# Raw gate weights of the first set in tiles of their own, asked for a pair ahead, in a hybrid decoder step

## The chip, the cores and the metric

The kernel runs on one core of a Trainium2 chip. The metric is the device time of one execution in microseconds; three executions were timed, and one more was taken with the hardware profiler. Engines are named as the profile does: PE is TensorE's matmul side (PEld its weight loads), DVE VectorE, ACT ScalarE, POOL GpSimd, SP SyncE, which here only issues transfers.

## What is computed

One decoder layer, for a prompt of 2048 tokens and for eight single-token samples that continue from given states. The mixer has two groups of four heads, retention (RET) and HGRN2:

```python
h = rmsnorm(x, norm_g)
p = (h @ w_in).astype(jnp.float32)                 # 1024 x 4096
rq, rk, rv, rg, hq, hf, hi, hgate = jnp.split(p, 8, axis=-1)
rq, rk = rotary(rq, pos), rotary(rk, pos) * RET_DK ** -0.5
o_ret, s_ret_new = chunked_decay_recurrence(rq, rk, rv, log_gamma, s_ret)
o_ret = head_rmsnorm(o_ret, ret_g) * silu(rg)
o_hg, s_hg_new = chunked_decay_recurrence(silu(hq), kin, hi, logf, s_hg)   # kin, logf from hf
o_hg = head_rmsnorm(o_hg, hg_g) * silu(hgate)
y = x + concatenate([o_ret, o_hg]) @ w_out
return rmsnorm(y, final_norm_g), new states
```

## The kernel before

All large products are made in fp32 as three passes over a high and a low part (`three`, L350: high x high, high x low, low x high). The first 570 us make the projections `rv`/`hi` (set 0), `rq`/`rg` (set 1) and `rk`/`hgate` (set 2). Each set goes over the prompt in eight chunks of 256 tokens; the loop counter `i` runs from 0 to 23 over all three sets, and the tiles of chunk i are named after it (`pv4a`, `s40h`). Chunks 0 and 1 are plain products. From chunk 2 on each chunk is a chain of seven products of half size with sums of operands (a Strassen-Winograd scheme): A11, A12, S2, S1, S3, S4, A22 against B11, B21, T2, T1, T3, B22, T4 (`CHAIN`). A product is 12 matmuls of 128x512. `v_pair` writes the chain, and the dictionary `after[n]` holds what is put in behind product n (n from 0 to 6; n - 0.5 is its middle). TensorE's order is exactly the order in which the code is written; the other engines' order is made by a scheduler, except where `behind(f)` ties the instructions of f to come after the last ones already issued on VectorE, ScalarE and SP.

The weights of sets 1 and 2 are used twice. While set 0 runs, the raw weights of set 1 (`w_1`, eight k-tiles `wgr` of 128x1024, in four pairs k and k + 4) are loaded by `wg_load` into buffers of the pool `rawp` (six buffers, tag `raw`, shared with the token tiles `xr` and the operand sums `S`); `wg_decode` multiplies them with the sample tokens (`four`, L590: four matmuls of 8x256 per k-tile into `pgd`); `w_sums` makes the T operands in place, and `wg_spool` stores these into `ws1T`, from where the next set fetches them. Set 1 does the same for set 2. Pair k has its place in chunk k + 2: load behind product 0, decode behind product 4 (5 in chunk 3).

Around these stand: `stats_load`/`stats_sum` (tiles `xn`: squares of the prompt rows on ScalarE for the norms; `stats_end` makes `rs_all` on POOL, `spread` transposes it on TensorE, `prs`, and copies it to `rb`); `tok_load`/`tok_ops` (tokens of the next chunk, scaled by `rb`, their high and low parts `ab_h`, `ab_l` and sums `S`); `decode_values` (the sample values from the raw weights `wvr` of set 0, in the plain chunk 0, behind its second and fourth k-pair); `wv_comb` (T operands of set 0, in place in `wvr`, so behind `decode_values`). In set 2 the retention recurrence runs inside the chain (`r_steps`, L797 on): `r_flip` transposes the keys `rk` (`pkt`), `r_score` and `r_update` follow. Later, in the output projection, `wd_at` places the steps of the decode output: `d_ms`, `d_rs` (VectorE's `do`, L1392), `d_tr` (TensorE's transpose `pdt`). `MOVE` shifts single score groups of the HGRN2 part in TensorE's order. The small matmuls `wu` (L84, L86) run while the first loads are under way. Tiles of the pool `vq` have one buffer per tag: `zh0`, `zl0`, `zh1`, `zl1` hold the A21 operands of chunks 0 and 1, `rk` and `rg` are otherwise used from the decode rotation of chunk 7 on.

Of the kernel before, what the change touches and what calls it, by code (L numbers as in the profile page):

```python
# [10 lines left out]
F32 = mybir.dt.float32  # L11
# [3 lines left out]
ALU = mybir.AluOpType  # L15
# [26 lines left out]
def step_kernel(ctx, tc, a, out):  # L42
# [42 lines left out]
    for n in range(12):  # L85
        pe.matmul(wu[:32, :16], ones[:, :32], ones[:, :16], start=True, stop=True)  # L86
# [415 lines left out]
    def w_sums(r0, r1):  # L502
        dve.tensor_tensor(r0[:, 0], r0[:, 1], r0[:, 0], op=ALU.subtract)
        dve.tensor_tensor(r0[:, 1], r1[:, 1], r0[:, 1], op=ALU.subtract)
        dve.tensor_tensor(r1[:, 1], r1[:, 1], r0[:, 0], op=ALU.subtract)
        dve.tensor_tensor(r1[:, 0], r1[:, 0], r1[:, 1], op=ALU.subtract)
        return ("T2", r1[:, 1]), ("T3", r0[:, 1]), ("T1", r0[:, 0]), ("T4", r1[:, 0])
# [6 lines left out]
    def wg_load(n, k):  # L514
        for kk in (k, k + 4):
            wr[kk] = rawp.tile([P, 2, GW], F32, tag="raw", name=f"wgr{n}{kk}")
            sp.dma_start(wr[kk].rearrange("p g n -> p (g n)"), a[f"w_{n}"][kk])
# [3 lines left out]
    def wg_decode(n, k):  # L521
        if n not in pgd:
            pgd[n] = ps_o.tile([P, 256], F32, tag="o", name=f"pgd{n}")
        for kk in (k, k + 4):
            four(pgd[n], xs[:, kk], wr[kk].rearrange("p a b -> p (a b)"), kk == 0, kk == KT - 1)
# [5 lines left out]
    def wg_decode_out(n):  # L531
        t, u = (vq.tile([NB, GW], F32, tag="vo", name=f"gd{n}{ty}", bufs=3) for ty in range(2))
        for ty, x in enumerate((t, u)):
            for m in range(2):
                j = 2 * ty + m
                act.activation(x[:, m * 256 : m * 256 + 256], pgd[n][32 * j : 32 * j + NB], AF.Copy)
        act.activation(u, u, AF.Silu)
        hd = NH * (n - 1)
        sp.dma_start(dg_dram[hd : hd + NH].rearrange("u b d -> b u d"), u.rearrange("b (u d) -> b u d", d=P))
        r = vq.tile([NB, GW], F32, tag="rv", name=f"gdr{n}")  # L540
        rotd = vq.tile([NB, GW], F32, tag="rk", name=f"rotd{n}")[:, :P]
        sp.dma_start(rotd, a["rotd"])
        turn(r, t, rotd, f"d{n}")
        dec_rot[n] = r
# [42 lines left out]
    def four(ps, x, w, first, last):  # L587

        for j in range(4):
            pe.matmul(ps[32 * j : 32 * j + x.shape[1]], x, w[:, j * 256 : j * 256 + 256], start=first, stop=last)  # L590
# [71 lines left out]
    for kk in range(4):  # L662
        for k in (kk, kk + 4):
            for ty in range(2):
                for c in range(2):
                    plain_k(0, pv0[c, ty], c, ty, k, k == 0, k == KT - 1)
        if kk % 2:
            for k in (kk - 1, kk, kk + 3, kk + 4):
                decode_values(k)
# [125 lines left out]
    def r_steps(p):  # L795
# [22 lines left out]
        if p < N_V:  # L818
            put(3, lambda: r_load(ca, "q"), lambda: r_load(ca, "v"))
            d = 0 if p else 0.5  # L820
            put(3.5 + d, lambda: r_flip(ca))
            put(4 + d if p else 6, lambda: r_load(ca, "g"))
# [85 lines left out]
    for i in range(2, n_tok):  # L908
# [30 lines left out]
        if i + 2 < N_V:  # L939
            after[1 if i == 2 else 2] += [lambda i=i: behind(lambda: stats_sum(i + 2, 0)), lambda i=i: stats_load(i + 2, 1)]  # L940
# [8 lines left out]
        if m < 3:  # L949
            if 2 <= j < 6:  # L950
                after[0] += [lambda m=m, k=j - 2: wg_load(m, k)]
                after[5 if i == 3 else 4] += [lambda m=m, k=j - 2: wg_decode(m, k), lambda m=m, k=j - 2: wg_spool(m, k)]
# [224 lines left out]
    MOVE = {(0, 0, 1): 0.065, (0, 1, 3): 0.065, (0, 2, 1): 0.065, (1, 0, 1): 0.125, (1, 3, 1): 0.11}  # L1177
# [699 lines left out]
    wd_at[2] += [(0, d_ms), (2, d_rs), (4, d_tr)]  # L1877
# [103 lines left out]
```

## Time and profile before

| | us |
|---|---|
| median of three runs | 1028.73 (1026.5 to 1032.09) |
| profiled execution, device time | 1030.97 |
| its span, first to last instruction | 1029.1 |
| PE busy | 1014.0 (99%) |
| DVE busy | 734.2 (71%) |
| ACT busy | 550.3 (53%) |
| POOL busy | 122.8 (12%) |
| data moved | 255.63 MB, mean 248 GB/s |

A busy PE means that matmuls are under way; since they overlap, the starts of two following matmuls tell more than their durations. In the timeline a row gives the start and the duration in us, then engine, line, operation and tiles; what stands in brackets is the idle time ahead of it and who ended it.

### The profile page before, as it was taken

How to read it: one execution, taken by the hardware profiler on the slowest of the kernel's cores; microseconds unless marked ns; L12 is line 12 of the kernel's file. 1: busy time of each engine (PE TensorE's matmuls, PEld its weight loads, DVE VectorE, ACT ScalarE, POOL GpSimd, SP SyncE). 2: the span in 40 equal slices, each digit the busy share in tenths (PEclk: the TensorE clock that was granted, in tenths of full speed). 3: DMA queues.
4: the chain of work that ended last, by engine and by line, in shares of the span. 5: the costliest groups of instructions: out<-in, count | busy, mean ns of one | idle time of the engine just before them, and what ended most of it. 6: DMA issues, size and time to landing. Idle time of an engine off the chain costs nothing.

```text
span 1029.1 us, 21541 instructions
## 1 busy us (share of the span) xinstructions
PE 1014.0 (99%) x8366; PEld 841.7 (82%) x8366; DVE 734.2 (71%) x1353; ACT 550.3 (53%) x1211; POOL 122.8 (12%) x231
## 2 busy tenths in 40 slices
PE   9999999999999999999999999999999999999997
PEld 7767778887778888888888899898888878878775
DVE  7887666888675885576666768768768576667886
ACT  7863435735434765555564665667556476433242
POOL 0200001000000101111111100111022112301122
PEclk9999999999999999999999999999999999999999
DMA  8699998878999965567766697555864496565652
GB/s 290 210 327 330 332 334 275 326 263 313 312 326 304 359 238 184 189 226 247 233 222 205 210 334 268 193 185 200 283 216 133 129 362 227 180 252 204 227 186 103
DMA packets 151271, 255.63 MB, mean 248 GB/s; under 512 B 11424, under 2 KB 79280, under 8 KB 151040
## 3 DMA queue, kind: packets, MB, share of 16 engines
q1 hardware_dynamic: 141408, 225.03, 64.7%
q0 software_dynamic: 7440, 24.76, 6.3%
q10 hardware_dynamic: 2320, 4.46, 1.2%
q8 instruction: 66, 1.08, 0.4%
q14 instruction: 37, 0.30, 0.1%
HBM read 166.51 MB, written 87.69 MB: 247 GB/s over the span
## 4 chain that ended last, share of the span: by engine, by line
PE 82%; DMA 4%; DVE 1%; issue 0%; SPq 0%; POOLq 0%; ACT 0%; POOL 0%; DVEq 0%; ACTq 0%
PE po L350 10%; PE pjqh L1032 9%; PE pjfh L1032 8%; PE py L1659 4%; PE plh L1246 2%; PE pur L741 1%; PE par L734 1%; PE puh L1115 1%; PE por L747 1%; PE por L749 1%; PE poh L1131 1%; DMA oT1h<-t_dramh 1%; PE poh L1133 1%; PE pv20a L350 1%; PE pv21a L350 1%; PE pv22a L350 1%
## 5 line engine op out<-in xcount | busy, mean ns | idle before, releaser
L1032 PE MATMUL pjfh<-xh,w_h 128*128 128x512 f32 (+2 forms) x160 | 59.4, 372 | 0.0
L1032 PE MATMUL pjqh<-xh,w_h 128*128 128x512 f32 (+2 forms) x160 | 58.9, 368 | 0.0
L1226 ACT ACTIVATE kepth<-kh 128x1024 f32<-128x1024 f32 x24 | 25.4, 1060 | 62.0 <-DVE kh L1216 62.0
L1032 PE MATMUL pjqh<-xh,w_l 128*128 128x512 f32 (+2 forms) x160 | 55.7, 348 | 0.0
L1032 PE MATMUL pjfh<-xh,w_l 128*128 128x512 f32 (+2 forms) x160 | 55.7, 348 | 0.0
L1032 PE MATMUL pjfh<-xl,w_h 128*128 128x512 f32 (+2 forms) x160 | 55.6, 348 | 0.0
L1032 PE MATMUL pjqh<-xl,w_h 128*128 128x512 f32 (+2 forms) x160 | 55.6, 347 | 0.0
L1216 DVE TENSOR_TENSOR kh<-kh,fph 128x512 f32<-128x512 f32 x48 | 33.4, 696 | 22.8 <-PE plh L1246 19.8
L118 DVE TENSOR_TENSOR ab_l<-xr,ab_h 128x512 fp32r<-128x512 f32 (+1 forms) x40 | 37.5, 954 | 11.6 <-ACT ab_h L117 11.6
L772 DVE SCALAR_TENSOR_TENSOR obr<-por,omr,rg 128x128 f32<-128x128 f32 x64 | 18.0, 344 | 33.3 <-POOL omr L764 28.2
L762 ACT ACTIVATE obr<-por 128x128 f32<-128x128 f32 x64 | 16.8, 277 | 44.4 <-PE por L749 40.6
L117 ACT ACTIVATE ab_h<-xr 128x512 fp32r<-128x512 f32 (+1 forms) x40 | 32.4, 838 | 11.3 <-DVE xr L302 11.3
L1032 PEld LDWEIGHTS pjqh<-xh,w_h 128*128 128x128 f32 x160 | 30.4, 190 | 4.8 <-issue 1.2
L1032 PEld LDWEIGHTS pjfh<-xh,w_h 128*128 128x128 f32 x160 | 30.2, 189 | 4.1 <-issue 0.4
L1032 PEld LDWEIGHTS pjqh<-xh,w_l 128*128 128x128 f32 x160 | 30.1, 188 | 4.1
L1032 PEld LDWEIGHTS pjfh<-xh,w_l 128*128 128x128 f32 x160 | 30.1, 188 | 4.0
L409 ACT ACTIVATE vo<-vo 128x512 f32<-128x512 f32 x32 | 20.1, 629 | 24.7 <-DVE vo L403 10.8
L1219 DVE TENSOR_TENSOR qqh<-qqh,fph 128x512 f32<-128x512 f32 x48 | 32.8, 683 | 0.0
L1032 PEld LDWEIGHTS pjqh<-xl,w_h 128*128 128x128 f32 x160 | 30.2, 189 | 3.0
L1032 PEld LDWEIGHTS pjfh<-xl,w_h 128*128 128x128 f32 x160 | 30.2, 189 | 2.7
L302 DVE SCALAR_TENSOR_TENSOR xr<-xr,g_in,rb 128x256 f32<-128x256 f32 x64 | 27.1, 480 | 7.3 <-DMA xr<-in_x_t 4.2
L1659 PE MATMUL py<-woh,oc_h 128*128 128x512 f32 x64 | 26.6, 415 | 0.0
(1839 smaller groups left out, 3335.0 us busy)
## 6 DMA issues: line engine op xcount, KB each, us to landing
xr<-a_dram SPq DMA_DIRECT2D x24, 512.0 KB
S<-s_dram SPq DMA_DIRECT2D x24, 512.0 KB
xn<-in_x_prompt SPq DMA_DIRECT2D x32, 256.0 KB
xr<-in_x_t SPq DMA_DIRECT2D x16, 512.0 KB
a_dram<-xr SPq DMA_DIRECT2D x16, 512.0 KB
s_dram<-S SPq DMA_DIRECT2D x16, 512.0 KB
wgr<-in_w SPq DMA_DIRECT2D x16, 512.0 KB
xr<-a_dram SPq DMA_DIRECT2D x32, 256.0 KB
```

The source lines that it names most:

```text
L117: act.activation(h, src, AF.Copy)
L118: dve.tensor_tensor(l, src, h.bitcast(F32), op=ALU.subtract)
L302: dve.scalar_tensor_tensor(r[:, k], r[:, k], g_in[:, kk : kk + 1], spread_to[i], op0=ALU.mult, op1=ALU.mult)
L350: pe.matmul(ps, xx, ww, start=(first and n == 0), stop=(last and n == 2), skip_group_check=more)
L409: act.activation(o, src, AF.Silu)
L772: dve.scalar_tensor_tensor(o[:, cc], po[:, h], ms[:, h : h + 1], rb_of[c, "g"][:, cc], op0=ALU.mult, op1=ALU.mult)
L1032: pe.matmul(ps, ww[:, kk], x[:, k, b0 : b0 + n], start=(k == 0 and i == 0), stop=(k == KT - 1 and i == 2),)
L1216: dve.tensor_tensor(kv[:, :, 0, :], kv[:, :, 0, :], two[:, :, 1:2].to_broadcast([P, nb, b]), op=ALU.mult)
L1219: dve.tensor_tensor(qv[:, :, 1, :], qv[:, :, 1, :], two[:, :, 0:1].to_broadcast([P, nb, b]), op=ALU.mult)
L1226: act.activation(ss[:, 512:], k[:, :HALF], AF.Copy)
L1246: pe.matmul(dst[32 * i : 32 * i + 32, c], kk, qq, start=True, stop=True)
L1659: pe.matmul(ps, o[:, kk], w[:, k % 4, i * 512 : (i + 1) * 512], start=(k == 0 and n == 0), stop=(k == KT - 1 and n == 2),)
```

## The change

The raw weights of set 1 no longer share `rawp` for most of their tiles. Pair 0 and pair 2 keep one `raw` buffer for their first k-tile, and the second goes as two halves into the tiles `rk` and `rg`; pairs 1 and 3 go as four halves into `zh0`, `zl0`, `zh1`, `zl1`. Pair 0 is loaded behind product 1 of chunk 2, each further pair behind product 5 of the chunk before its own, and all are decoded behind product 6. `w_sums`, `wg_decode` and `four` take a list of halves. Beside that: the gate store `dg_dram` of set 1 is issued by ScalarE instead of SP; `decode_values` runs in one block behind chunk 0; `stats_sum` and `stats_load` stand behind product 1 in all chunks; the first `r_flip` of set 2, with the first score and update, stands half a product later; `d_tr` moves from product 4 of output block 2 to product 0 of block 3; one score group of head 3 (`MOVE`) moves forward; three more small warm-up matmuls.

```diff
     def w_sums(r0, r1):
-        dve.tensor_tensor(r0[:, 0], r0[:, 1], r0[:, 0], op=ALU.subtract)
...
+        b11, b12, b21, b22 = (r[:, g] if hasattr(r, "shape") else r[g] for r in (r0, r1) for g in range(2))
+        dve.tensor_tensor(b11, b12, b11, op=ALU.subtract)
+        dve.tensor_tensor(b12, b22, b12, op=ALU.subtract)
+        dve.tensor_tensor(b22, b22, b11, op=ALU.subtract)
+        dve.tensor_tensor(b21, b21, b22, op=ALU.subtract)
+        return ("T2", b22), ("T3", b12), ("T1", b11), ("T4", b21)
...
     def wg_load(n, k):
-        for kk in (k, k + 4):
-            wr[kk] = rawp.tile([P, 2, GW], F32, tag="raw", name=f"wgr{n}{kk}")
-            sp.dma_start(wr[kk].rearrange("p g n -> p (g n)"), a[f"w_{n}"][kk])
+        for j, kk in enumerate((k, k + 4)):
+            if n == 1 and (j or k % 2):
+                tags = (f"zh{j}", f"zl{j}") if k % 2 else ("rk", "rg")
+                wr[kk] = [vq.tile([P, GW], F32, tag=t, name=f"wgr{n}{kk}{t}") for t in tags]
+                for g, r in enumerate(wr[kk]):
+                    sp.dma_start(r, a[f"w_{n}"][kk, :, g * GW : (g + 1) * GW])
+            else:
+                wr[kk] = rawp.tile([P, 2, GW], F32, tag="raw", name=f"wgr{n}{kk}")
+                sp.dma_start(wr[kk].rearrange("p g n -> p (g n)"), a[f"w_{n}"][kk])
...
-        sp.dma_start(dg_dram[hd : hd + NH].rearrange("u b d -> b u d"), u.rearrange("b (u d) -> b u d", d=P))
+        (act if n == 1 else sp).dma_start(dg_dram[hd : hd + NH].rearrange("u b d -> b u d"), u.rearrange("b (u d) -> b u d", d=P))
...
-    for n in range(12):
+    for n in range(15):
         pe.matmul(wu[:32, :16], ones[:, :32], ones[:, :16], start=True, stop=True)
...
-        if kk % 2:
-            for k in (kk - 1, kk, kk + 3, kk + 4):
+        if kk == 3:
+            for k in range(KT):
                 decode_values(k)
...
-            d = 0 if p else 0.5
+            d = 0 if p else 1
             put(3.5 + d, lambda: r_flip(ca))
-            put(4 + d if p else 6, lambda: r_load(ca, "g"))
+            put(4 if p else 6, lambda: r_load(ca, "g"))
...
-            after[1 if i == 2 else 2] += [lambda i=i: behind(lambda: stats_sum(i + 2, 0)), lambda i=i: stats_load(i + 2, 1)]
+            after[1] += [lambda i=i: behind(lambda: stats_sum(i + 2, 0)), lambda i=i: stats_load(i + 2, 1)]
...
-                after[0] += [lambda m=m, k=j - 2: wg_load(m, k)]
-                after[5 if i == 3 else 4] += [lambda m=m, k=j - 2: wg_decode(m, k), lambda m=m, k=j - 2: wg_spool(m, k)]
+                if m == 1:
+                    if j == 2:
+                        after[1] = [lambda m=m: behind(lambda: wg_load(m, 0))] + after[1]
+                    if j < 5:
+                        after[5] += [lambda m=m, k=j - 1: behind(lambda: wg_load(m, k))]
+                else:
+                    after[0] += [lambda m=m, k=j - 2: wg_load(m, k)]
+                after[6 if m == 1 else 4] += [lambda m=m, k=j - 2: wg_decode(m, k), lambda m=m, k=j - 2: wg_spool(m, k)]
...
-    MOVE = {(0, 0, 1): 0.065, (0, 1, 3): 0.065, (0, 2, 1): 0.065, (1, 0, 1): 0.125, (1, 3, 1): 0.11}
+    MOVE = {(0, 0, 1): 0.065, (0, 1, 3): 0.065, (0, 2, 1): 0.065, (1, 0, 1): 0.125, (1, 3, 1): 0.11, (0, 3, 1): -0.06}
...
-    wd_at[2] += [(0, d_ms), (2, d_rs), (4, d_tr)]
+    wd_at[2] += [(0, d_ms), (2, d_rs)]
+    wd_at[3] += [(0, d_tr)]
```

`four` and `wg_decode` index these lists instead of slicing one tile; the products are the same.

TensorE, end of chunk 2: before, the decode block of pair 0 (`pgd`, read from `wgr`) stands behind the fifth product, the second on `pv2a` with T3.

```order
L350 MATMUL pv2a<-T3h,s20l 128x512
L350 MATMUL pv2a<-T3h,s20h 128x512
L350 MATMUL pv2a<-T3l,s20h 128x512
L350 MATMUL pv2a<-T3h,s20l 128x512
L590 MATMUL pgd_922<-wgr_791,pk 8x256 x4
L590 MATMUL pgd_922<-wgr_793,pk 8x256 x4
L350 MATMUL pv2c<-B22h,s21h 128x512
L350 MATMUL pv2c<-B22l,s21h 128x512
```

In the change it stands behind the seventh product (T4), ahead of chunk 3, and reads the second k-tile from `wgr14rk` and `wgr14rg`.

```order
L350 MATMUL pv2a<-T4h,ab_h 128x512
L350 MATMUL pv2a<-T4l,ab_h 128x512
L350 MATMUL pv2a<-T4h,ab_l 128x512
L599 MATMUL pgd_969<-wgr_810,pk 8x256 x4
L599 MATMUL pgd_969<-wgr14rk,pk 8x256 x2
L599 MATMUL pgd_969<-wgr14rg,pk 8x256 x2
L350 MATMUL pv3a<-wv_h,ab_h 128x512
L350 MATMUL pv3a<-wv_l,ab_h 128x512
```

The block has moved two products later, with the same sixteen small matmuls.

SP's queue in the same chunk: before, the two loads of pair 0 stand ahead of the store of the first output (`v_dram`).

```order
L324 DMA s_dram_121<-S_2_708 128x1024
L263 DMA xn_761<-in_x_prompt 128x512
L517 DMA wgr_791<-in_w 128x1024
L517 DMA wgr_793<-in_w 128x1024
L344 DMA v_dram_95<-vo_808 128x512
L263 DMA xn_819<-in_x_prompt 128x512
L263 DMA xn_820<-in_x_prompt 128x512
L312 DMA a_dram_114<-xr_716 128x1024
```

In the change pair 0 has three loads and stands behind that store:

```order
L324 DMA s_dram_121<-S_2_711 128x1024
L263 DMA xn_764<-in_x_prompt 128x512
L344 DMA v_dram_95<-vo_807 128x512
L524 DMA wgr_810<-in_w 128x1024
L521 DMA wgr14rk<-in_w 128x512
L521 DMA wgr14rg<-in_w 128x512
L263 DMA xn_824<-in_x_prompt 128x512
L263 DMA xn_825<-in_x_prompt 128x512
```

Pair 1, which stood in chunk 3 before, follows in the same chunk, in four halves:

```order
L344 DMA v_dram_96<-vo_914 128x512
L263 DMA xn_942<-in_x_prompt 128x512
L263 DMA xn_943<-in_x_prompt 128x512
L344 DMA v_dram_96<-vo_939 128x512
L521 DMA wgr11zh_946<-in_w 128x512
L521 DMA wgr11zl_947<-in_w 128x512
L521 DMA wgr15zh_950<-in_w 128x512
L521 DMA wgr15zl_951<-in_w 128x512
L344 DMA v_dram_95<-vo_966 128x512
```

The first loads moved one store later, the second pair about half a chunk earlier.

VectorE at the start: before, the first in-place sums on the raw weights of set 0 (`wvr`, L503 to L506) stand among the splits of the later raw tiles.

```order
L118 TENSOR_TENSOR B12l_220<-wvr_267,B12h_218 128x512
L503 TENSOR_TENSOR wvr_223<-wvr_223 128x512
L503 TENSOR_TENSOR wvr_245<-wvr_245 128x512
L504 TENSOR_TENSOR wvr_223<-wvr_228,wvr_223 128x512
L118 TENSOR_TENSOR T1l<-wvr_223,T1h 128x512
L118 TENSOR_TENSOR wv_l<-wvr_289,wv_h 128x512
L118 TENSOR_TENSOR B12l_220<-wvr_289,B12h_218 128x512
L118 TENSOR_TENSOR wv_l<-wvr_291,wv_h 128x512
```

In the change they stand behind the splits of the tokens of chunk 1 (`x0r`), since TensorE reads the raw tiles for the decode values in one block:

```order
L481 SCALAR_TENSOR_TENSOR ab_l<-x0r_328,g_in,ab_h 128x128
L481 SCALAR_TENSOR_TENSOR a21l_207<-x0r_328,g_in,a21h_206 128x128
L481 SCALAR_TENSOR_TENSOR ab_l<-x0r_330,g_in,ab_h 128x2x128
L504 TENSOR_TENSOR wvr_226<-wvr_226 128x512
L481 SCALAR_TENSOR_TENSOR ab_l<-x0r_330,g_in,ab_h 128x2x128
L505 TENSOR_TENSOR wvr_226<-wvr_231,wvr_226 128x512
L504 TENSOR_TENSOR wvr_248<-wvr_248 128x512
L506 TENSOR_TENSOR wvr_231<-wvr_231,wvr_226 128x512
L118 TENSOR_TENSOR T1l<-wvr_226,T1h 128x512
```

All 32 operations of that kind now follow one another behind the decode block.

## Rows read from the trace of the kernel before

**Rows 1.** The page, busy time of each engine with its share and instructions.
```profile
PE 1014.0 (99%) x8366; PEld 841.7 (82%) x8366; DVE 734.2 (71%) x1353; ACT 550.3 (53%) x1211; POOL 122.8 (12%) x231
```

**Rows 2.** TensorE's waits: us in total, times, longest.
```profile
PE pgd L590 <- DMA wgr<-in_w: 2.7, 5, 0.7
PE pkt L726 <- DVE rk L375: 1.4, 1, 1.4
PE pdt L1396 <- DVE do L1392: 1.2, 1, 1.2
...
PE prs L288 <- POOL rs_all L114: 0.6, 1, 0.6
PE pv2b L350 <- DVE ab_l L118: 0.4, 1, 0.4
PE pv2a L350 <- ACT s L390: 0.3, 1, 0.3
```

**Rows 3.** The chain that ended last, in chunk 6: start, us, twelve matmuls.
```profile
143.63 2.72 PE pv6a L350 x12
```

**Rows 4.** Timeline of TensorE around the first and the last stalled decode block.
```profile
70.80 0.39 PE L350 MATMUL pv2a<-T3h,s20l 128*128 128x512 f32 x1
...
73.35 0.50 PE L350 MATMUL pv2c<-B22h,s21h 128*128 128x512 f32 x1
...
135.69 0.39 PE L350 MATMUL pv5a<-T3h,s50l 128*128 128x512 f32 x1
...
137.88 0.50 PE L350 MATMUL pv5c<-B22h,s51h 128*128 128x512 f32 x1
```

**Rows 5.** The same around an unstalled decode block of the second set.
```profile
236.80 0.39 PE L350 MATMUL pv10a<-T3h,s100l 128*128 128x512 f32 x1
...
238.09 0.50 PE L350 MATMUL pv10c<-B22h,s101h 128*128 128x512 f32 x1
```

**Rows 6.** Timeline of SP's issues, last pair of the first set.
```profile
128.22 1.32 SPq L517 DMA_DIRECT2D wgr<-in_w  x2
```

**Rows 7.** Timeline of TensorE, transpose of the norms in chunk 4.
```profile
104.67 0.39 PE L350 MATMUL pv4b<-wv_h,ab_l 128*128 128x512 f32 x1
...
105.63 0.43 PE L288 MATMUL prs<-ident,rs_all 128*128 128x128 f32 x2 [0.58 <-POOL rs_all L114]
```

**Rows 8.** Timeline of TensorE and VectorE, first transpose of keys in chunk 16.
```profile
361.85 0.39 PE L350 MATMUL pv16a<-T3h,s150l 128*128 128x512 f32 x1
363.65 0.63 PE L726 MATMUL pkt<-ident,rk 128*128 128x128 f32 x4 [1.41 <-DVE rk L375]
...
362.81 0.69 DVE L375 TENSOR_TENSOR rk<-t,t 128x512 f32<-128x512 f32 x1
```

**Rows 9.** Timeline of TensorE, transpose of the decode output.
```profile
914.50 0.39 PE L350 MATMUL po<-woh,op2S1l 128*128 128x512 f32 x1
916.07 0.24 PE L1396 MATMUL pdt<-ident,do 64*128 64x64 f32 x1 [1.18 <-DVE do L1392]
```

**Rows 10.** Timeline of VectorE and TensorE, first sums and second decode block.
```profile
19.59 1.28 DVE L503 TENSOR_TENSOR wvr<-wvr 128x512 f32<-128x512 f32 x2
20.79 0.68 DVE L504 TENSOR_TENSOR wvr<-wvr,wvr 128x512 f32<-128x512 f32 x1
...
31.49 1.91 PE L590 MATMUL pvd<-wvr,pk 128*8 128x256 f32 x32
```

**Rows 11.** Timeline of VectorE and TensorE, tokens of chunk 2 and its first matmul.
```profile
50.21 0.42 DVE L290 COPY rb<-prs 128x256 f32<-128x256 f32 x1 [1.34 <-PE prs L288]
...
53.86 0.69 DVE L118 TENSOR_TENSOR ab_l<-xr,ab_h 128x512 fp32r<-128x512 f32 x1 [0.72 <-ACT ab_h L117]
...
55.51 0.39 PE L350 MATMUL pv2a<-wv_h,ab_h 128*128 128x512 f32 x1
```

**Rows 12.** DMA from 60 to 140 us; stretch of chunk 6, DMA share second to last.
```profile
DMA packets 10211, 27.08 MB, mean 339 GB/s; under 512 B 1151, under 2 KB 1151, under 8 KB 10205
...
143.20:163.30 20.10, 20.10 (x91) 16.50 (x91) 13.24 (x24) 8.25 (x14) 1.08 (x3) 1.00 0.84 285
```

More of the change, by code (lines that the diff above doesn't have):

```diff
@@ L502, in w_sums @@
     def w_sums(r0, r1):
-        dve.tensor_tensor(r0[:, 0], r0[:, 1], r0[:, 0], op=ALU.subtract)
[L504 to L507, printed above, removed]
+        b11, b12, b21, b22 = (r[:, g] if hasattr(r, "shape") else r[g] for r in (r0, r1) for g in range(2))
[4 more added lines that the diff above has]
+        return ("T2", b22), ("T3", b12), ("T1", b11), ("T4", b21)
     def wv_comb(k):
@@ L524, in wg_decode @@
         for kk in (k, k + 4):
-            four(pgd[n], xs[:, kk], wr[kk].rearrange("p a b -> p (a b)"), kk == 0, kk == KT - 1)
+            halves = wr[kk] if isinstance(wr[kk], list) else [wr[kk][:, g] for g in range(2)]
+            four(pgd[n], xs[:, kk], halves, kk == 0, kk == KT - 1)
     def wg_spool(n, k):
@@ L589, in four @@
         for j in range(4):
-            pe.matmul(ps[32 * j : 32 * j + x.shape[1]], x, w[:, j * 256 : j * 256 + 256], start=first, stop=last)
+            ww = w[j // 2] if isinstance(w, list) else w[:, j // 2 * 512 : j // 2 * 512 + 512]
+            pe.matmul(
+                ps[32 * j : 32 * j + x.shape[1]], x, ww[:, j % 2 * 256 : j % 2 * 256 + 256], start=first, stop=last
+            )
     pvd = []
```

## The prediction

> **What bounds the kernel now.** I read the page's busy table first: TensorE is busy for 1014.0 us, 99% of the span [rows 1]. A change that takes no matmul out can only win from the 15 us in which TensorE stands, so the next view is TensorE's own list of waits [rows 2]. It has few: 2.7 us in five waits for the raw gate weights (`wgr`, read by the small decode products at L590), one wait each for a transpose of `rk` (1.4), a transpose of the decode output (1.2) and a transpose of the norms `rs_all` (0.6), and two at the start of the first chained chunk (0.4 and 0.3). The list shows idle time by modelled ends of matmuls; the price of a wait I take from starts in the timeline instead. Large matmuls follow each other at 2.72/12 = 0.227 us [rows 3]; what a stretch takes beyond that and beyond its normal small work is lost.
>
> **The change, part by part.**
>
> *Raw weights earlier (L514 to L525, L951).* Before, pair k of the first gate set is requested at the head of its chunk and consumed behind the fifth or sixth product of the same chunk. From the last large matmul ahead of a decode block to the first behind it took 2.55 us in the first block and 2.19 in the last stalled one; the stalled one between them took 2.65, by the same two rows of its place [rows 4]. In the second set the same 16 small matmuls cost 238.09 - 236.80 = 1.29 us unstalled [rows 5]. So the three stalls cost 2.55 + 2.65 + 2.19 - 3 x 1.29 = 3.5 us; the fourth block, pair 1's, did not wait. The last pair's requests stand on SP's queue from 128.22 on, and the block that waited for them ended at 137.88, so a transfer takes some 9 us from issue here [rows 4, 6]. After the change pair 0 is asked for some 2 us later on SP (one store now stands ahead of it) but consumed two products later (2 x 2.72 = 5.4 us), which leaves 3 us against waits below 1 us; pairs 1 to 3 are asked for a chunk (about 20 us) ahead. The new tiles (`rk`, `rg`, `zh0` to `zl1`) are free: the early chunks have finished with the `z` tiles when chunk 2 starts at 55.51 [rows 11], and the two sets alternate, so a load waits on SP only for the stores of the sums two pairs back. Such a wait may take a few us; the loads themselves have 20 us, but the `xn` loads stand behind them on SP (rival A). Saving 3.5 us, at least 2.5 (first and last block only), none if the queue is the limit (a rival below). The same 4 MB move either way. SP issues 14 loads instead of 8.
>
> *The statistics one product earlier (L940).* The transpose of `rs_all` that waits stands in chunk 4; the last squares that it needs stand on ScalarE behind the first copy of `pv4a`, which waits for TensorE. The order after puts them ahead of that copy. Loss before: 105.63 - 104.67 - 0.23 = 0.73 us [rows 7]. I take 0.7, bounds 0 and 0.7. It also pulls `xn` squares forward on ScalarE for the later chunks; if an `xn` load is late, the PSUM copies queue behind it.
>
> *The first transpose of keys half a product later (L820, L821).* Before, it stood 363.65 - 361.85 - 0.23 = 1.57 us for VectorE's rotation, which ends at 362.81 + 0.69 = 363.50 [rows 8]. Six large matmuls (1.36 us) now come ahead of it, so TensorE arrives at 363.44 on that clock and waits at most 0.2. The score behind it moves by the same six, so its distance stays. Saving 1.3, bounds 1.0 and 1.57.
>
> *The decode output's transpose two products later (L1877).* Loss before: 916.07 - 914.50 - 0.23 = 1.34 us [rows 9]. It moves by some 36 large matmuls (8 us); VectorE's product for it stays where it is. Saving 1.3; no lower bound below 1.2 that the rows suggest.
>
> *Decode values in one block (L667), three more tiny warm-up matmuls (L85).* The work is the same, one switch fewer: nothing. But the first four raw tiles are now read by TensorE until about 31 us, so VectorE's in-place sums on them cannot begin at 19.59, as they did, but at about 29.9 [rows 10] (the second block of 32 small matmuls began at 31.49; the 64 now begin 1.9 earlier, at 29.6). 32 operations (16 sums, 16 low parts) at 0.60 us each are 19.3 us, so the end is 49.2 if nothing waits. Before, `rb`, which follows them, ran at 50.21 waiting for TensorE, and the first block's low part was done at 54.55 for matmuls that start at 55.51 (the third of these reads it) [rows 11]. If ScalarE makes VectorE wait for about 2 us, the low part is done at 56.5 and TensorE loses about 0.5. On the other side SP now issues more of the statistics loads ahead of the two 512 KB token loads, so ScalarE may wait less, and both waits of this place (0.4 and 0.3 of idle time, [rows 2]) can go; with the restart behind each, which cost the decode blocks up to a third more than the idle time, that is some 1 us. I take a loss of 0.5; bounds: a gain of 1.0 and a loss of 2.0, the whole lateness. The warm-up adds six records of a 32x16 product; the second real matmul waits for its split behind it anyway: nothing.
>
> *Score group of head 3 earlier (`MOVE`), gate store on ScalarE's queue (L539).* No wait of [rows 2] lies at either, so neither gives anything; if the score group came too early, it would cost one wait of the size of [rows 8] at worst. The store leaves SP; what it gives is sequencer time on a queue that nobody waits for there. The Trainium skill ("DMA: Bandwidth & Descriptors", section "Issuing engines are not separate DMA queues") says the same: transfers run on the same 16 engines whoever issues them. By it, too, nothing is to be had.
>
> **Sum.** -3.5 - 0.7 - 1.3 - 1.3 + 0.5 = -6.3 us. The profiled execution took 1030.97 us, 1.87 beyond its span and 2.24 above the median of the three runs; taken off the median, 1028.73 - 6.3 = **1022.4 us**, 0.6% less. Half a per cent (5.1 us) is about what a measurement of this kernel can tell from no change, so the forecast stands just beyond it.
>
> **Rivals.**
>
> *A. The DMA queue is the limit, and the stalls move.* From 60 to 140 us the queue moved 27.08 MB at 339 GB/s; in chunk 6 behind it, at 285 GB/s, the DMA engines' share is 0.84 [rows 12], so 339 is close to all they do with such transfers (285/0.84 = 339). Without the stalls the stretch takes about 4.2 us less (3.5 + 0.7) and wants 27.08/75.8 = 357 GB/s. If it can't have them, token or `xn` loads come late and TensorE or ScalarE waits for these instead, until the slack behind 143 us. For it: the load. Against: pairs 1 to 3 now have 20 us, tokens are used a chunk after they are asked for, and backlog of a few us drains at 0.84. Price: the 4.2 us, leaving -2.1: 1026.6. Chance 0.17.
>
> *B. The start is late.* As bounded above, 2.0 instead of 0.5: -4.8, 1023.9. For it: the sums that began at 19.59 cannot fill VectorE's time there any more. Chance 0.18.
>
> *C, slower. Shorter rows slow the queue itself.* Six of the eight raw loads become pairs of 256 KB with 2 KB rows instead of 4 KB. That is 768 packets more on 10211 [rows 12], 7.5%. If each packet had a fixed price, the rate would fall; the other terms give 2.1 us, so the kernel gains nothing once the stretch takes 82.1 us instead of 80 (330 GB/s), and is slower by 0.5% at 87.2 us (311 GB/s). At 300 GB/s it takes 90.3 us, 8.2 more than it can: 1036.9. Against: the stretch already consists of 256 KB and 512 KB transfers and reaches 339. Chance 0.04. The Trainium skill speaks for C ("DMA: Bandwidth & Descriptors", section "Rules for kernel authors": 1 MiB and more per transfer; "Perfetto Trace Analysis", section "DMA Optimizations": going from 2 KB to 4 KB can improve throughput a lot). The first page's section "Bandwidth" gives 341 GB/s for a single 1 MB transfer; this trace has 339 with transfers of a quarter to a half of that in a full queue. By the rule the time would go towards C's 1036.9, by the row halving costs nothing, and I go by the row.
>
> *D. The change doesn't reach the waits*: the loads land no earlier because `behind` and the scheduler hold them. The order speaks against it (pair 1's loads stand half a chunk earlier): 0.03. Then the 3.5 us stay: 1028.73 - 2.8 = 1025.9.
>
> **Chances.** Forecast 0.58, A 0.17, B 0.18, C 0.04, D 0.03. Three runs before spread from 1026.5 to 1032.1, so a median is good to some 2 us: of the forecast about 0.70 falls beyond 5.1 us, of B 0.45, of A 0.2. That gives faster 0.41 + 0.08 + 0.03 = 0.52, slower 0.04, the same 0.44. Range: best 1028.73 - 6.3 - 1.5 (the start gains 1.0) = 1020.9, less some 2 for the median: 1018.5; top end A plus 1: 1027.6.
>
> **What the profile after would show.** The five waits for `wgr` gone and each decode block near 1.3 us; no wait of `prs` at chunk 4; `pkt` at most 0.2; `pdt` none; TensorE idle down by some 5 us. VectorE's sums starting at about 30 us, `rb` at 50 to 52, and a wait of `pv2a` of 0 to 1 us. A shows as new waits of TensorE for ScalarE or VectorE behind DMA `xr` or `xn` between 80 and 143 us; C as a rate clearly below 339 GB/s in that stretch. The prediction is wrong if TensorE's waits go and the span does not follow, or if waits appear behind 143 us, where I priced nothing.

## The result and the profile after

The changed kernel takes 1031.47 us (median of 22 runs, 1027.37 to 1037.52), the kernel before in the same comparison 1028.35 us (22 runs): 1.0031 times as long, 95% interval 1.0019 to 1.0043. That is some 3 us slower, less than the half per cent that the prediction called telling, but clear by the interval; 1022.4 us was forecast and 1027.6 was the top of the range.

The execution whose trace was read first took 1037.52 us, 6 us above the median. So the changed kernel was profiled once more (1030.74 us; run e12 below), and the kernel before as well (1025.78 us; run e5). TensorE's waits in this second profile of the changed kernel (us in total, times, longest):

```profile
PE pv8a L350 <- ACT s L390: 1.8, 1, 1.8
PE plh L1263 <- issue: 1.2, 1, 1.2
PE wu L84 <- POOL ones L78: 1.1, 1, 1.1
PE pv2c L350 <- ACT p L390: 1.0, 1, 1.0
PE pv2a L350 <- ACT ab_h L117: 0.6, 1, 0.6
PE par L745 <- DMA rq<-qt_dram: 0.4, 1, 0.4
PE pv2a L350 <- ACT s L390: 0.3, 1, 0.3
PE pv2b L350 <- DVE ab_l L118: 0.2, 1, 0.2
```

Against [rows 2] every wait that the change was to remove is gone: none for `wgr`, `prs`, `pkt` or `pdt`. Others stand in their place. Two of the new ones are the largest that both profiles of the changed kernel share: `pv8a` in chunk 8, the first chunk of set 1, and `pv2c` in chunk 2. In the first profile of the changed kernel the place of `pv8a` cost more; TensorE's timeline there:

```profile
185.45 0.49 PE L350 MATMUL pv8b<-wv_h,ab_h 128*128 128x512 f32 x1 [0.72 <-ACT wv_h L117]
...
186.71 0.50 PE L350 MATMUL pv8b<-wv_l,ab_h 128*128 128x512 f32 x1 [0.77 <-DVE wv_l L118]
...
190.21 0.79 PE L350 MATMUL pv8a<-T2h,s70h 128*128 128x512 f32 x1 [2.06 <-ACT s L390]
```

A stretch of the same profile (us; busy times of PE, PEld, DVE, ACT and POOL; granted clock, DMA share, GB/s):

```profile
190.00:195.00 5.00, 4.79 (x15) 3.84 (x16) 5.00 (x5) 4.26 (x6) 0.00 (x0) 0.67 1.04 411
```

There are three waits, 3.55 us together, and from the end of the last of them on TensorE has a piece at the lower clock level (1.2 GHz instead of 2.4; the granted clock is 0.92 on average from 189 to 190 us, 0.50 from 190 to 193 and 0.67 from 190 to 195). It is no single case: the mean granted clock of the whole execution is 0.996 or less in 12 of the 22 executions of the changed kernel and in 1 of the 116 of the kernel before that ran beside the experiments.

Because TensorE runs nearly without a gap, the account is best kept by the time from the first matmul of one chunk to the first of the next. Worked out from TensorE's timelines, in us, where the four profiles differ:

| stretch | before, 1030.97 | before, 1025.78 | changed, 1037.52 | changed, 1030.74 |
|---|---|---|---|---|
| start to chunk 2 | 55.51 | 56.04 | 56.47 | 56.08 |
| chunk 2 | 23.43 | 20.92 | 23.88 | 23.93 |
| chunk 4 | 22.64 | 21.82 | 20.50 | 20.50 |
| chunk 5 | 21.38 | 21.37 | 20.50 | 20.50 |
| chunk 8 | 20.10 | 20.09 | 25.95 | 22.19 |
| chunk 16 | 23.99 | 22.72 | 22.45 | 22.44 |
| chunk 17 to output projection (`py`) | 467.22 | 466.93 | 467.63 | 468.87 |
| output projection on `po`, to its end | 120.97 | 119.77 | 121.47 | 119.84 |

The mean of the two profiles of before against the second of the changed kernel: chunks 4 and 5 gain 1.7 + 0.9, chunk 16 gains 0.9, the output projection 0.5; chunk 2 loses 1.75, chunk 8 2.1 (5.9 in the first profile of the changed kernel), the start 0.3. So the gains are 4.0 us instead of 6.8 (the stalled decode block of chunk 2 is not among them: what it gave back is part of that chunk's net loss), and they are lost again at the start, in chunk 2 and in chunk 8 even in the milder of the two executions. Of the 1.8 between chunk 17 and the output projection 0.4 are for `par` and 1.2 at `plh`; a run without any of the weights' part (e11) has 1.6 at `plh` too, so I count that to the spread of executions, which is not shown further.

The two profiles of before also differ from each other, and in places that the prediction summed. TensorE's waits in the second:

```profile
PE pgd L590 <- DMA wgr<-in_w: 1.0, 2, 0.7
PE prs L288 <- POOL rs_all L114: 0.8, 2, 0.6
```

And its timeline at `pkt` and `pdt`:

```profile
359.47 0.39 PE L350 MATMUL pv16a<-T3h,s150l 128*128 128x512 f32 x1
359.98 0.63 PE L726 MATMUL pkt<-ident,rk 128*128 128x128 f32 x4
...
910.62 0.39 PE L350 MATMUL po<-woh,op2S1l 128*128 128x512 f32 x1
910.94 0.28 PE L1396 MATMUL pdt<-ident,do 64*128 64x64 f32 x1
```

`pkt` stands 0.51 - 0.23 = 0.28 us there instead of the 1.57 of [rows 8], `pdt` 0.1 instead of 1.34 [rows 9], and `wgr` 1.0 instead of 2.7 [rows 2].

### The profile page after: what moved, and what is told of

Same layout as the page of the kernel before. It is cut to its first block, busy times and chain, and to the rows that moved or that the text cites. A ratio compares the mean times of both kernels' runs of the same rounds, so it can differ in the third digit from the quotient of the medians.

```text
span 1035.7 us, 21567 instructions
## 1 busy us (share of the span) xinstructions
PE 1017.9 (98%) x8372; PEld 843.1 (81%) x8372; DVE 734.6 (71%) x1353; ACT 551.2 (53%) x1211; POOL 126.9 (12%) x231
## 5 line engine op out<-in xcount | busy, mean ns | idle before, releaser
L409 ACT ACTIVATE vo<-vo 128x512 f32<-128x512 f32 x32 | 20.1, 628 | 23.7 <-DVE vo L403 10.5
```

The lines of the kernel that those rows point to most:

```text
L409: act.activation(o, src, AF.Silu)
```

## The experiments

Medians are of 11 or 12 runs each (6 for e15; e5 and e12 are one execution each), with those of before taken beside them (1027.96 to 1028.12, 23 to 35 runs); the ratio to before is given with its 95% interval. Edits are shown against the changed kernel unless said otherwise.

**e1: the statistics put back.**
```diff
-            after[1] += [lambda i=i: behind(lambda: stats_sum(i + 2, 0)), ...
+            after[1 if i == 2 else 2] += [lambda i=i: behind(lambda: stats_sum(i + 2, 0)), ...
```


> The changed kernel with one edit undone: the squares for the statistics stand again behind step 2 of a chunk (step 1 in chunk 2). Theory T (set turnover): the changed kernel loses at the start of set 1, because the first loads of set 1's weights are issued at 165.85 us instead of 157.54; part of that comes from ScalarE's order in chunk 6, where the split of chunk 7's first block stands behind two outputs of chunk 6, so that SP waits 6.8 us to store that block with the loads queued behind it. Undone, ScalarE's order is that of before; T expects that store's wait to go, the loads some 3 us earlier, TensorE's waits between 180 and 200 us down from 3.55 us to 1 to 2, and 2 to 3 us less than the changed kernel, less 0.7 for the wait for prs that returns: 1029 to 1030. Rival R (the loss is at the start and in the tail, and the stall at 185 to 190 us belongs to one execution): 1031 to 1032.


1029.47 us, 1.0015 (1.0004 to 1.0027). T's number. In its profile chunk 8 takes 20.11 us, no wait is left there, and three waits for `prs` of 0.5 us stand in chunks 4, 5 and 6. The first loads come only 1.7 us earlier than in the changed kernel's first profile (164.11 instead of 165.85 us), the third, though, 4.5 (165.55 instead of 170.00). T had expected waits of 1 to 2 us to stay.

**e2: the raw weights put back** (`wg_load` all in the raw ring at step 0, `wg_decode` at step 4 or 5).
```diff
+                after[0] += [lambda m=m, k=j - 2: wg_load(m, k)]
+                after[5 if i == 3 else 4] += [lambda m=m, k=j - 2: wg_decode(m, k), ...
```


> The changed kernel with the raw weights of set 0 as before (all in the raw ring, loaded at step 0 of their chunk, used at step 4 or 5). T: the first load for set 1 stands again ahead of the stores of s_dram on SP, no wait of TensorE between 180 and 200 us; the three stalls behind pgd return (3.5 us); 1028.35 + 1.4 (start, as measured at 79 us in the changed kernel) - 0.6 (prs) - 1.4 (pkt) - 1.8 (pdt) = about 1026. R: the start and the tail still lose, the pgd stalls return: 1031 to 1034.


1028.16 us, 0.9999 (0.9987 to 1.0011). The stall in chunk 8 is gone (20.09) and TensorE waits 3.1 us for `wgr`, as T said; but the 1026 is missed. The gains for `pkt` and `pdt` that T had taken from one profile are not in the median.

**e3: the start put back.**
```diff
-        if kk == 3:
-            for k in range(KT):
+        if kk % 2:
+            for k in (kk - 1, kk, kk + 3, kk + 4):
```


> The changed kernel with the decode values in two blocks again and 12 small warm-up matmuls. T: the stall between 180 and 200 us stays; only the 1.4 us by which chunk 3 starts later are won back: about 1030. R: the start is the larger part of the loss: 1028 or less.


1029.93 us, 1.0016 (1.0001 to 1.0030). T's number. Chunk 2 takes 21.73 us instead of 23.9, chunk 8 still 25.07 with waits of 0.7 and 2.1.

**e4: the loads of set 1 on another queue.**
```diff
-                sp.dma_start(r, a[f"w_{m}"][kk, :, c0 : c0 + GW].rearrange(...))
+                (pool if m == 1 and op in ("B11", "B21") else sp).dma_start(r, a[f"w_{m}"][kk, ...
```


> The changed kernel with the four loads of set 1's first two operands (B11, B21) on GpSimd's queue instead of SP's, so that they are no longer queued behind the stores of chunk 7's blocks and sums. T: the first is issued at about 152 to 155 us instead of 165.85, lands before the split wants it, no wait of TensorE above 0.3 us between 180 and 200 us, granted clock 1.00 there, and the time falls by the 5.8 us that the changed kernel loses between 181 and 189 us in its profile, somewhat less at its median: 1026 to 1028. R: no difference, 1031.


1031.60 us, 1.0033 (1.0021 to 1.0045): T missed. Chunk 8 is clean (20.10), but now chunk 7 takes 22.07 instead of 19.04. ScalarE's timeline of this run shows why:

```profile
169.91 0.76 ACT L544 ACTIVATE gd<-pgd 8x256 f32<-8x256 f32 x2 [5.29 <-DMA v_dram<-vo]
172.48 0.77 ACT L544 ACTIVATE gd<-pgd 8x256 f32<-8x256 f32 x2 [1.80 <-DMA v_dram<-vo]
173.27 0.60 ACT L390 ACTIVATE u<-pv7a 128x512 f32<-128x512 f32 x1
```

The gates' tiles `gd` wait until stores of `v_dram` are done, and `u`, for which TensorE waits 2.2 us, stands behind them. SP does not issue the three stores ahead of `gd` later: they come 1.95, 2.64 and 3.89 us behind the start of chunk 7, in the changed kernel's second profile 1.95, 2.63 and 3.81, and there `gd` waits 1.51 us. So they finish later here, where the two loads of B21 on GpSimd's queue are issued at 1.50 and 2.32; that these hold them up is not shown. To move the loads alone clears chunk 8 and moves the stall.

**e5: the kernel before again**, and **e6: before with only the late edits** (against before):
```diff
-            d = 0 if p else 0.5
+            d = 0 if p else 1
-    wd_at[2] += [(0, d_ms), (2, d_rs), (4, d_tr)]
+    wd_at[2] += [(0, d_ms), (2, d_rs)]
+    wd_at[3] += [(0, d_tr)]
```


> The kernel before once more, for a second profile: the one that the prediction was read from took 1030.97 us, 2.9 above the median of 35 runs (1028.12). Theory U (an untypical profile): one or more of the stalls that the prediction summed (pgd 3.5, prs 0.7, pkt 1.3, pdt 1.3) are shorter or gone in an execution near the median. Theory V (typical stalls): all of them are there again at the same size, and the 2.9 us lie elsewhere.

> The kernel before with only the late edits of the change: the turns and gate loads of the first retention head half a step later, the transpose pdt a pair later, and the one move in the gated pass. V: the stalls of 1.3 us at pkt and 1.3 us at pdt go, 1028.1 - 2.6 = 1025.5. U: they were not there at the median, 1028.


e5 took 1025.78 us, its rows stand above: U, though this execution lies 2.2 us below the median beside it, about as far as the first lies above. e6 took 1027.11 us, 0.9995 (0.9982 to 1.0008): V's 2.6 us are not there; what there is is below 1.9 us and may be nothing.

**e7: start and statistics both put back** (the edits of e1 and e3), and **e8: the same, statistics moved in two chunks.**
```diff
+            after[1 if i < 4 else 2] += [lambda i=i: behind(lambda: stats_sum(i + 2, 0)), ...
```


> The changed kernel without the block of decode values, without the three more warm-up matmuls and with the statistics where they were before: the new tiles for raw weights, the gates' store on ScalarE's queue and the late edits stay. Theory T: no pgd stall, no stall at the start of set 1 (the run with the statistics put back had none), and the start of before: chunk 2 in 21.7 us as with the start put back, instead of 23.4 to 23.9. From the 1029.93 of the run with the start put back, less the 5.0 us that chunk 8 lost there in its profile, plus 1.5 for three waits of 0.5 behind rs_all: 1026 to 1027, the first version below before. If it is no faster than before (1028), the stalls removed were no gain even without their side effects.

> As the run before, with the squares of the statistics moved to step 1 in chunks 2 and 3 only (2 and 5 steps earlier in the chunks before ScalarE's order of chunk 6 is touched). T: the wait for prs in chunk 4 is gone as in the changed kernel (0.5 to 0.7 us) and ScalarE's order in chunk 6 is that of before: 0.5 us below the run without the move. Rival: no difference.


e7: 1028.71 us, 1.0008 (0.9998 to 1.0019), not the 1026 to 1027 of T; by the expectation's own alternative, the stalls removed were no gain here. The stall in chunk 8 is nearly gone (20.83), but TensorE waits 1.8 us for `prs` in chunk 4, 0.5 in chunks 5 and 6 and 1.1 for `p` in chunk 2. The 1.8 is this execution's: e1 and e9, with the same places for statistics and weights, have 0.5 in chunk 4 too. e8: 1027.26 us, 0.9995 (0.9986 to 1.0004): the wait in chunk 4 is gone, and the median is 1.45 lower, more than T gave it.

**e9: the weights' part alone** (before with only that part).


> The kernel before with only the raw weights' part of the change (own tiles, loads a pair ahead, the product of the decode rows at the chunk's end); the gates' store stays on SP. Theory T (the stall removed uncovers the next late thing): the pgd waits go, but prs waits 1.8 us in chunk 4 and 0.5 in chunks 5 and 6, and pv2c waits 0.4 to 1.0 us for p: 0 to 1.5 us above before. Rival W (the weights' part is a gain of its own and the loss of 1.6 between the run with late edits alone and the one with weights, gates' store and late edits comes from the store): 1.3 + 0.9 us below before, about 1026.


1027.42 us, 0.9996 (0.9986 to 1.0005): no measurable gain, and at most 1.4 us. TensorE's waits in its profile say where it went:

```profile
PE prs L288 <- POOL rs_all L114: 1.6, 3, 0.5
PE wu L84 <- POOL ones L78: 1.1, 1, 1.1
PE pv2c L350 <- ACT p L390: 0.7, 1, 0.7
```

No wait for `wgr`; 1.6 + 0.7 = 2.3 us of others. Kernels with the old weights' part waited 1.0, 2.0, 2.6, 2.7 and 3.1 us for `wgr` (e5, e6, e11, [rows 2], e2), 2.3 on average. Not all of the others are new: the two profiles of before wait 0.6 and 0.8 us for `prs`, so the removed waits uncovered 1.5 to 1.7. W's gain of 2.2 isn't there; one of half a microsecond may be.

**e10: the decode product back in the middle of its chunk** (against e8).
```diff
-                after[6 if m == 1 else 4] += [lambda m=m, k=j - 2: wg_decode(m, k), ...
+                after[5 if i == 3 else 4] += [lambda m=m, k=j - 2: wg_decode(m, k), ...
```


> The run with the statistics moved in two chunks (1027.26), with the product of the decode rows at step 4 of its chunk again (5 in chunk 3) instead of step 6. T: the product stands again between T3 and B22 and covers ScalarE's turn of p (1.0 us of waiting in chunk 2): about 1026.5. But ScalarE's split of chunk 7's first block then stands behind p in chunk 6 (before: ahead of it), ahead of the output it stood behind in the changed kernel: T expects a late start of set 1 to return in part, 0 to 2 us of waiting between 170 and 200 us, which would eat that gain.


1027.32 us, 0.9994 (0.9982 to 1.0005), as e8. No wait for `p` in chunk 2 (21.70 instead of 23.35), as T said, but `prs` waits 1.4 us in chunk 6; chunk 8 is clean (20.12), against T's fear; T's 1026.5 is missed.

**e11: late edits and two chunks' statistics, nothing of the weights.**


> The kernel before with the late edits and the squares of the statistics at step 1 in chunks 2 and 3, and nothing of the weights: T: the wait for prs in chunk 4 (0.58 us in both profiles near the median) goes, the pgd waits stay: 0.5 us below the run with the late edits alone, 1026.6. Rival: no difference from before.


(The edits of e6 and e8.) 1027.88 us, 1.0001 (0.9990 to 1.0012): no difference; T's 1026.6 is missed.

**e12: the changed kernel again.**


> The changed kernel once more, for a second profile: T: the waits of pv8b and pv8a between 180 and 200 us are there again with 3 to 4 us and a granted clock below 1.00 behind them, chunk 2 takes 23.4 to 23.9 us again, and the 1.2 us that the tail lost to a late load of or in the first profile is not there. U2: the stall at the start of set 1 is that of one execution and is gone.


1030.74 us. Chunk 2 takes 23.93 us and the tail's 1.2 are not there, as T said. The wait at `pv8a` is there with 1.8 us, but less than T said, and the granted clock stays 1.00. U2 falls.

**e13: the decode product in the middle and the old start (the edits of e10 and e3), all statistics early**; **e14: the same with the gates' store on SP**; **e15: the changed kernel with only that store on SP.**
```diff
-        (act if n == 1 else sp).dma_start(dg_dram[hd : hd + NH]...
+        sp.dma_start(dg_dram[hd : hd + NH]...
```


> The changed kernel with the start of before (two blocks of decode values, 12 warm-up matmuls) and the product of the decode rows at step 4 of its chunk (5 in chunk 3), and the statistics moved in all four chunks as in the change. Here ScalarE's split of chunk 7's first block stands ahead of the output that it stood behind in the changed kernel, and the first load for set 1 ahead of the stores of s_dram on SP. Theory T: no stall at the start of set 1, no wait for prs (2.0 us in the run with two chunks moved), no wait for p in chunk 2: 1027.3 - 2.0 = 1025.3, the first version measurably below before. Rival X (the early statistics themselves, not ScalarE's order, bring the stall): a wait of 1.8 to 3.5 us between 180 and 200 us, 1029 to 1031.

> The run before with the gates' store on SP's queue as in the kernel before. If the store on ScalarE's queue matters (the run with weights and SP's store took 1027.4, the one with weights, ScalarE's store and late edits 1028.7), it differs by 0.5 to 1.3 us; T expects no difference, 1025.3, since no instruction of the chain waits for this store before the tail.

> The changed kernel with only the gates' store back on SP. T: no difference from the changed kernel (1031), the stall at the start of set 1 stays. Rival Y (the store on ScalarE's queue makes the late start of set 1): 1028 and no wait between 180 and 200 us.


e13: 1027.21 us, 0.9989 (0.9977 to 1.0000), the best version here, 0.75 us below before and at the edge of what the interval tells. X falls: all statistics are early and chunk 8 takes 20.12 us. T's 1025.3 is missed, since a new wait stands in chunk 6: `pv6a` waits 0.9 us for `vo`, which now stands behind the split on ScalarE (chunk 6 takes 20.51, 1.0 more than before), and the first decode block still waits 1.0 us for a load in that profile. e14: 1027.45 us, 0.9992 (0.9978 to 1.0005): no difference from e13, as T said, but its 1025.3 is missed again. e15: 1034.35 us, 1.0054 (1.0033 to 1.0075): both theories missed it. The store on ScalarE's queue does not make the stall; back on SP it makes it worse: chunk 8 takes 29.16 us. A stretch of it:

```profile
190.00:195.00 5.00, 4.34 (x10) 3.47 (x11) 5.00 (x5) 4.39 (x6) 0.00 (x0) 0.50 0.93 315
```

## Why the prediction was wrong

The forecast was 6.3 us less, the measurement 3.1 us more. Two steps failed: the sum had no term for the loads of set 1, which the change made late, and it booked the removed stalls as time won. By the medians the weights' part gives 0.6 us (e9) where 3.5 were booked and the late edits 0.9 (e6) where 2.6 were; of the 3.1 us the old start takes back 1.5 (e3) and the old statistics 2.0 (e1), or 0.8 and 1.2 once the other is put back already (e7 against e1 and e3). Each of these is good to about 1 us.

**The stall at the start of set 1 was not priced.** The prediction priced no loss behind 143 us, though it named waits there as a sign of being wrong, and of the earlier statistics it named only the PSUM copies that might queue behind late `xn` loads. What happened is in the order of ScalarE and SP. ScalarE in chunk 6 of the kernel before (second profile):

```profile
152.29 0.63 ACT L117 ACTIVATE ab_h<-xr 128x512 fp32r<-128x512 f32 x1 [1.99 <-DVE xr L302]
152.83 0.58 ACT L390 ACTIVATE p<-pv6c 128x512 f32<-128x512 f32 x1
...
155.45 0.58 ACT L402 ACTIVATE vo<-pv6a 128x512 f32<-128x512 f32 x1
```

And of the changed kernel (second profile):

```profile
153.15 0.60 ACT L390 ACTIVATE p<-pv6c 128x512 f32<-128x512 f32 x1 [2.12 <-PE pv6c L350]
155.87 0.60 ACT L402 ACTIVATE vo<-pv6a 128x512 f32<-128x512 f32 x1 [2.12 <-PE pv6a L350]
156.37 0.62 ACT L117 ACTIVATE ab_h<-xr 128x512 fp32r<-128x512 f32 x1
```

The split `ab_h` of chunk 7's first block (its high part) has moved behind two outputs for which ScalarE waits; VectorE's low part and the sums for chunk 7 follow it, and SP stores the blocks and sums later. SP's issues from there on, before:

```profile
152.29 2.51 SPq L312 DMA_DIRECT2D a_dram<-xr  x2
154.89 0.39 SPq L569 DMA_DIRECT2D wg1B<-in_w  x1
...
161.80 0.51 SPq L569 DMA_DIRECT2D wg1B<-in_w  x1
162.36 0.61 SPq L542 DMA_DIRECT2D rotd<-in_rotd  x1
163.03 0.38 SPq L569 DMA_DIRECT2D wg1B<-in_w  x1
```

And changed:

```profile
152.47 6.39 SPq L312 DMA_DIRECT2D a_dram<-xr  x2
...
165.52 1.12 SPq L577 DMA_DIRECT2D wg1B<-in_w  x2
166.74 0.35 SPq L550 DMA_DIRECT2D rotd<-in_rotd  x1
169.23 0.34 SPq L344 DMA_DIRECT2D v_dram<-vo  x1
169.62 3.06 SPq L577 DMA_DIRECT2D wg1B<-in_w  x4
```

The row that decides is the third load of `wg1B`, the first half of the second operand, B21. Before, it is issued 163.03 - 160.38 = 2.65 us behind the start of chunk 7; in the changed kernel it stands on SP behind a store of `v_dram` that waits for VectorE, 169.62 - 161.11 = 8.5 us behind that start. From there the chain is plain in ScalarE's timeline. Before (second profile; chunk 8 starts at 179.43 us):

```profile
174.68 1.05 ACT L117 ACTIVATE wv_h<-wg1B 128x1024 fp32r<-128x1024 f32 x1
178.32 1.06 ACT L117 ACTIVATE wv_h<-wg1B 128x1024 fp32r<-128x1024 f32 x1 [2.58 <-DMA wg1B<-in_w]
...
183.55 0.58 ACT L390 ACTIVATE s<-pv8a 128x512 f32<-128x512 f32 x1
```

And changed (second profile; chunk 8 starts at 180.15 us):

```profile
178.05 1.06 ACT L117 ACTIVATE wv_h<-wg1B 128x1024 fp32r<-128x1024 f32 x1 [2.20 <-DMA wg1B<-in_w]
181.64 1.06 ACT L117 ACTIVATE wv_h<-wg1B 128x1024 fp32r<-128x1024 f32 x1 [2.52 <-DMA wg1B<-in_w]
...
186.87 0.59 ACT L390 ACTIVATE s<-pv8a 128x512 f32<-128x512 f32 x1
```

Before, ScalarE waits for the second half of B21 alone; in the changed kernel it waits for both, then does four more splits and a copy, and only then copies `s`, 6.7 us behind the start of chunk 8 instead of 4.1, and `pv8a` waits 1.75 us for it. All the runs that issue these loads on SP agree with the distance of the third load: it is 2.1 to 2.9 us with the old weights' part, 2.6 to 4.1 in e1, e7, e8, e9, e10, e13 and e14, where chunk 8 takes 20.1 to 20.8 us; 8.5 to 8.6 in both profiles of the changed kernel and in e3, where it takes 22.2 to 26.0; and 11.3 in e15, where the gates' store stands ahead of the loads as well and it takes 29.2. The first two loads are late along with the third (4.4 and 5.0 us behind that start against at most 1.2 and 3.0 in the others); but in e15 they stand where they stand in the changed kernel, and only the loads from the third on are later, so it is these that lengthen the stall. e4, which takes the four loads off SP, clears chunk 8. ScalarE's order goes with it: the split stands behind both outputs, `p` and `vo`, in the changed kernel, e3, e4 and e15, and ahead of `vo` in all the others. e1 and e2 show that neither the statistics nor the weights' part does it alone, e13 that early statistics do no harm when the order stays good. Why the order came out so is not shown further than that: it follows the statistics and the weights together, and small shifts elsewhere undo it.

In time this place cost 2.0 us by e1 (1.6 by the ratios), net of the `prs` waits that came back there: chunks 4 to 6 take 21.23, 21.24 and 20.22 us in e1 against 20.50, 20.50 and 19.58, 2.1 us. Without them it is some 4.

**The stalls were sized from one execution.** The terms -3.5, -1.3 and -1.3 were read from a profile 2.24 us above the median of its three runs. The prediction noted that and subtracted the terms from the median all the same. `pkt` and `pdt` are worth 0.3 and 0.1 in the second profile; e9, which has both in their old places and was profiled near its median, has 0.3 at `pkt` and no wait at `pdt`. e6 bounds both together at less than 1.9 us at the median. The waits for `wgr` were not untypical: three executions with the old weights' part near the median have 2.0, 2.6 and 3.1 us of them (e6, e11, e2). The prediction's lower bound for them was summed wrongly: the first and the last block alone give 2.55 + 2.19 - 2 x 1.29 = 2.2 us, not 2.5.

**The raw weights: the stall went, the time did not.** Its mechanism was right: the loads are in time and no block waits. But the wait was not the last thing late at its place. Behind it stood `p` on ScalarE in chunk 2, which the decode block in the middle of the chunk had covered (1.0 us in e8, none in e10, where the block is back), and `rs_all` on GpSimd, for which chunks 5 and 6 wait 0.5 us each in e1, e7 and e9; that the time lost before had given it room is argued, not shown. The prediction said of each stall what it cost, not what would be late next.

**The start.** +0.5 was taken, with a loss of 2.0 as the bound (rival B). e3 puts it at 1.5 us in the time. The prediction took ScalarE to hold VectorE up for about 2 us; the row of `rb` in the second profile of the changed kernel, and the sums ahead of it:

```profile
50.82 0.68 DVE L507 TENSOR_TENSOR wvr<-wvr 128x512 f32<-128x512 f32 x1
...
52.64 0.68 DVE L118 TENSOR_TENSOR T4l<-wvr,T4h 128x512 fp32r<-128x512 f32 x1
53.24 0.41 DVE L290 COPY rb<-prs 128x256 f32<-128x256 f32 x1
```

It runs 3 us later than in [rows 11] (50.21), where it waited for TensorE, and outside the 50 to 52 that the prediction named. That holds in all profiles: `rb` starts at 52.0 to 53.6 us without a wait in the six with the new start, at 50.2 to 51.0 behind a wait for TensorE in the eleven with the old one. TensorE pays for it at up to three places of chunk 2 (0.6, 0.2 and 0.3 in the list of waits); the fourth there, 1.0 at `pv2c`, comes from the decode block that moved, since e7, e8 and e9 have it with the old start and e2 has none with the new one and the block in its old place. The 0.2 and 0.3 are not the new start's alone: the old start has waits there in three profiles of eleven, that of [rows 2] among them. The low part of the first block is done at 56.75 us, close to the 56.5 of the prediction. So the mechanism was right and the size off by 1.0 us, inside its bounds.

**The statistics.** The wait of `prs` in chunk 4 is gone, as predicted, and its size was right: chunk 4 takes 21.23 us in e1 and e9, with the wait, and 20.50 in the changed kernel.

**The gates' store.** "Neither gives anything" was wrong in the changed kernel: by e15 it saves some 2.4 us there (1.0054 against 1.0031; the intervals overlap), because SP would wait for the gates with the loads of set 1 queued behind. In the good order (e14 against e13) it gives nothing. The rule of the Trainium skill that the prediction cited ("DMA: Bandwidth & Descriptors", section "Issuing engines are not separate DMA queues") speaks of the sequencer's time to initiate a DMA. What held the loads up is not that time (0.30 us for this store) but the 2.45 us between the store ahead of it and its own issue, while SP waited for the gates; the two rows of e15 on SP:

```profile
168.10 0.35 SPq L344 DMA_DIRECT2D v_dram<-vo  x1
170.90 0.30 SPq L547 DMA_DIRECT2D dg_dram<-gd  x1
```

**The rivals.** A did not happen: no wait behind `xn` or `xr` loads shows in chunks 3 to 6 of the changed kernel. Its premise, that 339 GB/s is close to all that the queue does, was low: in single slices of 2 us between 60 and 140 us the kernel before moved up to 422 GB/s. C neither: chunks 3 to 5 take 20.5 us without a stall, and from 60 to 140 us the changed kernel (second profile) keeps the rate with more packets than in [rows 12]:

```profile
DMA packets 11303, 27.21 MB, mean 340 GB/s; under 512 B 1272, under 2 KB 1272, under 8 KB 11297
```

D is refuted by the waits that are gone. The slower case that came true was none of them.

## What to carry to other kernels

Before a stall is subtracted, ask what stands just behind it: e9 removed some 2.3 us of waits and uncovered 1.5 to 1.7 us of others. Size a stall from two profiles, or from one at the median, above all when it is a microsecond out of a thousand. And where one engine issues most transfers, read the order of its queue at the places that the edit does not touch: a load's lateness was decided by which store, waiting for its data, stood ahead of it.

## What was unexpected in the hardware

The clock took a part in the loss. Chunk 8 in the second and the first profile of the changed kernel, in e3 and in e15 (columns as above):

```profile
180.15:202.34 22.19, 20.44 (x93) 16.33 (x92) 19.76 (x23) 16.69 (x22) 0.55 (x1) 1.00 0.82 325
180.49:206.44 25.95, 22.40 (x93) 17.30 (x92) 21.30 (x24) 18.57 (x25) 0.55 (x1) 0.93 0.75 291
178.04:203.11 25.07, 22.34 (x94) 17.38 (x92) 21.32 (x24) 17.67 (x25) 0.55 (x1) 0.93 0.77 300
179.02:208.18 29.16, 25.38 (x94) 18.75 (x93) 21.32 (x24) 18.56 (x25) 0.55 (x1) 0.82 0.70 258
```

The waits in them are 1.75 us (one), 3.55 (three), 2.73 (two) and 3.79 (five); against the 20.1 us of the kernel before they lose 2.1, 5.9, 5.0 and 9.1 us. At 0.50 the matmuls of e15 follow each other at 0.43 us (eleven from 191.26 to 195.95) instead of 0.227 [rows 3]. So by an estimate from these rows a clock of 0.93 over 25.95 us costs some 0.07 x 25.95 = 1.8 us, over 25.07 us 1.8 too, and one of 0.82 over 29.16 us 5.2. Waits and clock together then come to 1.8, 5.4, 4.5 and 9.0, close to what was lost. In e15, whose waits are hardly longer than those of the first profile, the lower level holds from 187 to 196 us (0.50), in the first profile from 190 to 193. So the loss grew faster than the waits did.
